# Second MLP product: running sums kept in PSUM banks instead of SBUF accumulators, and weight sums made by adding transfers

## The chip, the core and the metric

The kernel runs on one core of a Trainium2 chip. The metric is the device time of the kernel in microseconds (us); the kernel before was timed in three runs. A profile of one execution was taken beside these runs; its span goes from the first to the last instruction.

The engines are named as the profile names them: PE (TensorE) multiplies matrices into eight PSUM banks of 128 x 512 float32; DVE (VectorE) and ACT (ScalarE) read PSUM and SBUF; POOL (GpSimd) reads SBUF alone; SP issues transfers. Each engine works through its instructions in the order in which the program wrote them.

## The reference

One encoder layer over 1024 tokens of width 1024. What matters here is its last line, the squared-ReLU MLP with 4096 hidden channels:

```
u = RMSNorm(x)
...
x = x + m @ W_o
h = rms_norm(x, norm2_g) @ w_mlp_in            # 1024 x 4096
x = x + square(relu(h)) @ w_mlp_out            # back to 1024 x 1024
```

## The kernel before

All products run in float16 pieces: each operand is split into a high and a low part (ACT casts the high part, DVE computes the low part as the rest), and three passes (high x high, high x low, low x high) are summed in PSUM.

**The second MLP product.** The 4096 hidden channels are taken in four *chunks* s = 0 to 3. Each chunk is a product of 2 x 2 blocks by the Winograd form of Strassen's scheme: seven products o = 0 to 6 instead of eight. The running number is n = 7 s + o, 0 to 27. Each product has four *units* j = 0 to 3 of 128 tokens, and a unit is 12 matmuls of 512 columns into one PSUM bank (`unit`, line 210). The scheme's result blocks need sums of the products: with P0 to P6 the seven products in the order of the loop, X11 gets P0 + P2; X12 gets -(P0 + P1), P4 and P6; X22 gets -(P0 + P1 + P3) and P4; X21 gets P0 + P1 + P3 and P5.

**The operands (`prep2`).** For each product, operand set `ops` is prepared ahead in one of three buffers: ACT casts the activations `hf` (L1765, 128 x 2048), DVE makes their low part (L1767), ACT casts the weights (L1770, two of 128 x 1024), DVE makes their low parts (L1776, two of 128 x 1024). A `gate` holds the preparation of product n until the units of product n - 3 are in the program, so L1765 of product n waits until PE is done with product n - 3, and all of this preparation stands in DVE's order ahead of the reads of product n - 2. The preparation of product n also issues, on SP, the load of `hf` for product n + 3 (L1711). The weights of the seven products are w11, t2, w21, t3, t1, t4, w22: some are blocks of the weight matrix, some are sums of blocks, and the sums are made on POOL, as `tensor_tensor` additions: T2 = w12 + w22 + w11 (L1739, L1740), then in place w11 += w12 after product 0 is prepared (L1781), w12 += w22 after product 1 (L1785), T2 += w21 after product 3 (L1789).

**The results.** A unit's result is read out by its `post`, which the program writes after the matmuls of the *next* unit. The banks rotate: `anybank` hands out eight banks in turn, so seven other units stand between two that write the same bank. For o in 0, 1 and 3 the product goes to an accumulator in SBUF (`acc`, three of 128 x 4 x 512): in chunk 0 ACT copies it there (L1864), in chunks 1 to 3 DVE adds it there (L1866). For o in 2, 4, 5 and 6 DVE adds it straight into X1 (L1875), twice for o = 4. In chunk 3, `combine` adds the three accumulators to one another and into X1 on DVE and POOL (L1837 to L1846), and `SP.dma_start` writes the finished blocks out.

**What stands around the start of this stage.** The first MLP product (`quad` q = 0 to 15) ends just before. The last work on its hidden channels, `h_done` for q = 15, is Relu (L1623) and Square (L1625) on ACT, then on POOL the sums (L1345), and on DVE the maximum of a small row (L1640) and the steps of `pow2` (L108 to L113). The program writes L1640 before the first unit of product 0; the first three steps of `unit`'s loop then write L108, L110 and, between them, the two L1776 of product 2.

Of the kernel before, what the change touches and what calls it, by code (L numbers as in the profile page):

```python
# [10 lines left out]
F32 = mybir.dt.float32  # L11
# [3 lines left out]
AF = mybir.ActivationFunctionType  # L15
OP = mybir.AluOpType
# [36 lines left out]
def encoder_block(ctx: ExitStack, tc: tile.TileContext, x, weights, cols, gqk, rel, masks, out):  # L53
# [12 lines left out]
    def bank(tag):  # L66
        return psum.tile([128, 512], F32, name="ps_" + tag, tag=tag, bufs=banks[tag])
# [3 lines left out]

    rc = [0]

    def anybank():
        rc[0] += 1
        return bank("dsodsods"[rc[0] % 8])


    sc = base.tile([128, 512], F32, name="sc")
    sci = sc.bitcast(I32)  # L80
    area = {"keep": [0, 0, 144], "prep": [144, 144, 240], "tmp": [240, 240, 512]}

    def cols_of(kind, n):
        a = area[kind]
# [32 lines left out]
    fg, bg = [], []  # L117
# [9 lines left out]
    def step(n=1):  # L127
        for _ in range(n):
            for g in list(fg):
                if not advance(g):  # L130
                    fg.remove(g)
# [72 lines left out]
        V.tensor_scalar(sc[:, out], bk[:, 0:1], floor, None, op0=OP.max)  # L204
        yield

    def unit(mms, post=None, steps=0, ticks=0):

        for ps, l, r, a, b in mms:
            T.matmul(ps, l, r, start=a, stop=b)  # L210
        units[0] += 1
        work[0] += len(mms) * mms[0][0].shape[-1]
        settle()
        if post:
            late.append(post)
        for i in range(max(steps, ticks)):
            if i < steps:
                step()
            if i < ticks:
                tick()  # L220
# [228 lines left out]
    def group(ps, pairs):  # L449
        return [(ps, l, r, i == 0, i == len(pairs) - 1) for i, (l, r) in enumerate(pairs)]  # L450
# [318 lines left out]
    for n, (kind, b) in enumerate(todo):  # L769
# [6 lines left out]
        def post(ps=ps, kind=kind, n=n, ch=ch):  # L776
            fg.append(qk_vec(ps, ch.inv, kind, q16[n]))
# [840 lines left out]
    def h_done(q, c0=0, c1=512, wait1=0, wait2=0):  # L1618

        f = AS[q] if c1 < 512 else AS.pop(q)  # L1620
        v = f[:, :, c0:c1]
        yield from wait(wait1)
        A.activation(v[:, 0:4], v[:, 0:4], AF.Relu)  # L1623
        yield
        A.activation(v[:, 0:4], v[:, 0:4], AF.Square, scale=sc[:, c1w[q].inv],  # L1625
                     accum_out=sc[:, at(bsum[q // 4], 4 + q if c1 < 512 else q % 4)])
        yield
        yield from wait(wait2)
        if q > 1:
            yield from sums(v, G)  # L1630
        else:
            for _ in sums(v, V):
                pass
        if c1 < 512:
            return
        SP.dma_start(HS[q // 4][:, :, q % 4], f)
        live.remove(q)
        if q % 4 == 3:
            m = tmp()
            V.tensor_reduce(sc[:, m], sc[:, bsum[q // 4]], axis=AX, op=OP.max)  # L1640
            yield
            yield from pow2(m, 14, *R[q // 4])
            r_ready[q // 4] = True

    def quad(q, c0=0, c1=512):
# [69 lines left out]
    def prep2(s):  # L1715
# [19 lines left out]
            yield  # L1735
        sums = sum_of(sm)
        T2 = later["t2"]()
        for i in range(2):
            G.tensor_tensor(T2[:, i], w12[i], w22[i], op=OP.add)  # L1739
            G.tensor_tensor(T2[:, i], T2[:, i], w11[i], op=OP.add)  # L1740
        yield
        if s == 0:
            yield from gate(17)
# [3 lines left out]
        sw, inv = yield from scale_of(sums, 0)  # L1747
        fw = keep()
        mul(iR, sw, fw)
        c2[s].inv = inv  # L1750
        yield
        for o, (f, name) in enumerate(ORDER):
            n = 7 * s + o
            i = 16 + n
            yield from gate(i)
            pool, tag = TAGS[i % 3]
            if n > 1:
                OPS[i] = pool.tile([128, 2, 2, 2048], F16, name="ops", tag=tag)
            P = OPS[i]
            while ("h", n) not in later:  # L1760
                yield
            if 1 < n < 25:
                h_load(n + 3)
            hf = later.pop(("h", n)).rearrange("p k t -> p (k t)")
            A.activation(P[:, 1, 0], hf, AF.Copy, scale=sc[:, Rs])  # L1765
            yield
            V.scalar_tensor_tensor(P[:, 1, 1], hf, sc[:, Rs], P[:, 1, 0], op0=OP.mult, op1=OP.subtract)  # L1767
            w = {"w11": w11, "t1": w11, "t3": w12, "w21": w21, "w22": w22}.get(name) or [T2[:, i] for i in range(2)]
            for i2 in range(2):
                A.activation(P[:, 0, 0, 1024 * i2:1024 * i2 + 1024], w[i2], AF.Copy, scale=sc[:, fw])  # L1770
            yield
            while i == 17 and pe_done[0] < 16:
                yield
            for i2 in range(2):
                sl = slice(1024 * i2, 1024 * i2 + 1024)
                V.scalar_tensor_tensor(P[:, 0, 1, sl], w[i2], sc[:, fw], P[:, 0, 0, sl], op0=OP.mult, op1=OP.subtract)  # L1776
                yield
            ready.add(i)
            if name == "w11":
                for i2 in range(2):  # L1780
                    G.tensor_tensor(w11[i2], w11[i2], w12[i2], op=OP.add)  # L1781
                yield
            elif name == "t2":
                for i2 in range(2):
                    G.tensor_tensor(w12[i2], w12[i2], w22[i2], op=OP.add)  # L1785
                yield
            elif name == "t3":
                for i2 in range(2):
                    G.tensor_tensor(T2[:, i2], T2[:, i2], w21[i2], op=OP.add)  # L1789
                yield  # L1790
            elif name == "t1":
                done[0] += 4
                load_upto(done[0] + 5)
                if s < 3:
                    w2x_load(s + 1)
                    bg.append(prep2(s + 1))
            yield
# [22 lines left out]
    p4.close()  # L1820
    p5 = ExitStack()
    w5p = later["pool"] = p5.enter_context(tc.tile_pool(name="p5", bufs=1, reuse_waits="tile"))
    acc = {i: w5p.tile([128, 4, 512], F32, name=f"acc{i}") for i in (1, 6, 7)}
    t2 = w5p.tile([128, 2, 1024], F32, name="t2")
    later["t2"] = lambda: t2
    later["junk"] = w5p.tile([128, 2048], BF16, name="junk")

    combined = set()
    PLACE = {2: ((0, 0),), 4: ((4, 512), (0, 512)), 5: ((4, 0),), 6: ((0, 512),)}
    SUM = {0: 1, 1: 6, 3: 7}  # L1830

    def combine(j, o):

        x11, x12, x21, x22 = X1[:, j, :512], X1[:, j, 512:], X1[:, j + 4, :512], X1[:, j + 4, 512:]
        a1, a6, a7 = (acc[i][:, j] for i in (1, 6, 7))
        if o == 0:
            G.tensor_tensor(x11, x11, a1, op=OP.add)  # L1837
        elif o == 1:
            V.tensor_tensor(a6, a6, a1, op=OP.add)
            yield  # L1840
            G.tensor_tensor(x12, x12, a6, op=OP.subtract)
        else:
            V.tensor_tensor(a7, a7, a6, op=OP.add)
            yield
            G.tensor_tensor(x22, x22, a7, op=OP.subtract)
            V.tensor_tensor(x21, x21, a7, op=OP.add)  # L1846
        combined.add((j, o))
        yield

    for n in range(28):  # L1850
        s, o = n // 7, n % 7
        need(16 + n)
        P = OPS.pop(16 + n)
        inv = c2[s].inv
        for j in range(4):
            bk = anybank()
            for c, m in ((0, 256), (256, 256)) if n == 27 and j == 3 else ((0, 512),):
                ps = bk[:, c:c + m]

                def post(ps=ps, j=j, o=o, s=s, c=c, m=m, inv=inv):  # L1860
                    if o in SUM:
                        t = acc[SUM[o]][:, j]
                        if s == 0:
                            A.activation(t, ps, AF.Copy, scale=sc[:, inv])  # L1864
                        else:
                            V.scalar_tensor_tensor(t, ps, sc[:, inv], t, op0=OP.mult, op1=OP.add)  # L1866
                        if s == 3:
                            fg.append(combine(j, o))
                        return
                    before = {2: 0, 4: 3, 5: 3, 6: 1}[o]  # L1870
                    while s == 3 and (j, before) not in combined:
                        step()
                    for b, d in PLACE[o]:
                        t = X1[:, b + j, d + c:d + c + m]
                        V.scalar_tensor_tensor(t, ps, sc[:, inv], t, op0=OP.mult, op1=OP.add)  # L1875
                    if s == 3:
                        b, d = PLACE[o][0]
                        r = (b + j) * 128
                        SP.dma_start(out[r:r + 128, d + c:d + c + m], X1[:, b + j, d + c:d + c + m])

                unit(group(ps, [(P[:, 1, sa, 512 * k + 128 * j:512 * k + 128 * j + 128],
                                 P[:, 0, sw, 512 * k + c:512 * k + c + m]) for k in range(4) for sa, sw in PASSES]),
                     post, 2, 4)
        pe_done[0] = 17 + n
    settle()
    p5.close()
# [57 lines left out]
```

## Time and profile before

| | |
|---|---|
| device time, median of 3 runs (lowest, highest) | 1208.2 us (1207.58, 1208.48) |
| the profiled execution: span | 1205.3 us |
| what lies between its span and the median of the runs | 2.9 us |
| first matmul of the second MLP product | 911.12 us |
| last unit of it (24 matmuls of 256 columns) | starts at 1198.69 us |
| busy in the span | PE 1188.0, DVE 938.7, ACT 759.8, POOL 433.1 us |

The page lists no device time of the profiled execution apart from its span; sums are made against the span, and the 2.9 us are carried along to speak of the median.

In a row of the timeline stand: start and length in us, engine, line, operation, output and inputs with their shapes, the number of merged instructions, and in brackets how long the engine sat idle before and what released it. In a row of the table by windows stand: the window, its length, then for PE, PEld, DVE, ACT and POOL the busy us and the number of instructions, then the granted clock of PE, the share of the DMA engines and GB/s.

### The profile page before, as it was taken

Reading aid. Unit: us, or ns where it says so; the run is one execution under the profiler, and the core shown is the slowest. Engines: PE = TensorE matmul, PEld = TensorE weight load, DVE = VectorE, ACT = ScalarE, POOL = GpSimd, SP = SyncE. Lnnn points to the kernel's source line nnn. Section 1 sums busy time; section 2 is a strip of 40 time slices with the busy share of each in tenths; the row PEclk is TensorE's granted clock in tenths of the full one; section 3 lists DMA queues with packets and bytes.
Section 4 is the critical chain, followed back from the end, with each engine's and each line's share of the span. In section 5 each row is a group of like instructions: output and inputs, shape, how many; then the busy total and the mean of one; then the engine's idle time right before and its main releaser. Section 6 shows DMA issues by size and latency. Waiting matters only on the chain.

```text
span 1205.3 us, 17076 instructions
## 1 busy us (share of the span) xinstructions
PE 1188.0 (99%) x6294; PEld 573.8 (48%) x6294; DVE 938.7 (78%) x1759; ACT 759.8 (63%) x1183; POOL 433.1 (36%) x280
## 2 busy tenths in 40 slices
PE   6999999999999999999999999999999999999998
PEld 4444445555444444444467444444444444444444
DVE  7777988988368787877878655545548999999997
ACT  7766679867554545337779778678676744746440
POOL 1640011222311112001004465565567471553662
PEclk9999999999999999999999999999999999999999
DMA  7766657676542211224386545445465925334202
GB/s 264 151 213 141 140 119 130 133 146 123 103 123 65 67 56 53 70 93 187 57 155 183 182 159 192 149 139 193 145 247 201 352 97 217 129 138 194 105 35 105
DMA packets 171012, 173.36 MB, mean 144 GB/s; under 512 B 131504, under 2 KB 132016, under 8 KB 166832
## 3 DMA queue, kind: packets, MB, share of 16 engines
q1 hardware_dynamic: 170352, 168.07, 47.9%
q10 hardware_dynamic: 576, 4.19, 0.8%
q8 instruction: 49, 0.80, 0.3%
q14 instruction: 35, 0.29, 0.1%
HBM read 102.51 MB, written 37.75 MB: 116 GB/s over the span
## 4 chain that ended last, share of the span: by engine, by line
PE 73%; DVE 9%; ACT 1%; issue 1%; DMA 1%; DVEq 0%; ACTq 0%
PE ps_d L210 26%; PE ps_s L210 23%; PE ps_o L210 16%; PE ps_d L1039 6%; DVE w_s L1163 2%; PE ps_o L1016 1%; PE ps_s L959 1%; DVE sg L1279 1%; DVE P L999 1%; DMA u2T<-v 1%; DVE sz L973 1%; ACT w_s L1167 0%; DVE sc L317 0%; DVE m L1281 0%; ACT sg L1245 0%
## 5 line engine op out<-in xcount | busy, mean ns | idle before, releaser
L210 PEld LDWEIGHTS <-ops 128*128 128x128 f16 x1356 | 132.4, 98 | 157.3
L210 PEld LDWEIGHTS <-w 128*128 128x128 f16 x1368 | 132.8, 98 | 140.0 <-DMA u2T<-v 0.6
L1039 PE MATMUL ps_d<-uT,w_ws 128*128 128x512 f16 x528 | 123.7, 379 | 0.1
L210 PE MATMUL ps_d<-ops 128*128 128x512 f16 (+1 forms) x528 | 118.3, 374 | 0.0
L1765 ACT ACTIVATE ops<-hf,sc 128x2048 f16<-128x2048 f32 x26 | 52.0, 2000 | 97.9 <-PE ps_o L210 35.2
L210 PE MATMUL ps_s<-ops 128*128 128x512 f16 x492 | 112.9, 379 | 0.0
L1152 POOL TENSOR_TENSOR tsum<-raw 128x512 f32<-128x512 f32 x28 | 46.0, 1658 | 149.6 <-ACT raw L1138 141.6
L1345 POOL TENSOR_TENSOR as<-as 128x512 f32<-128x512 f32 x56 | 77.5, 1384 | 39.3 <-ACT as L1625 36.0
L210 PEld LDWEIGHTS <-w_s 128*128 128x128 f16 x588 | 56.8, 98 | 69.4 <-DVE w_s L1163 1.9
L210 PE MATMUL ps_d<-u2x,w 128*128 128x512 f16 (+1 forms) x360 | 80.0, 372 | 0.0
L210 PEld LDWEIGHTS <-uT 128*128 128x128 f16 x504 | 49.0, 98 | 59.6 <-DMA uT<-u 0.8
L1039 PEld LDWEIGHTS <-w_ws 128*128 128x128 f16 x528 | 51.2, 98 | 54.5 <-DVE cv L861 0.4
L210 PE MATMUL ps_o<-ops 128*128 128x512 f16 x336 | 77.1, 379 | 0.0
L1767 DVE SCALAR_TENSOR_TENSOR ops<-hf,sc,ops 128x2048 f16<-128x2048 f32 x26 | 74.0, 2846 | 3.7 <-ACT ops L1765 3.7
L210 PE MATMUL ps_o<-u2T,w 128*128 128x512 f16 (+1 forms) x324 | 71.7, 371 | 0.0
L1138 ACT ACTIVATE raw<-raw,sc 128x256 f32<-128x256 f32 x172 | 71.0, 493 | 0.8 <-DMA raw<-in_weights 0.7
L1152 POOL TENSOR_TENSOR gsum<-raw 128x512 f32<-128x512 f32 x14 | 19.0, 1376 | 133.0 <-issue 72.8
L1167 ACT ACTIVATE w<-raw,sc 128x512 f16<-128x512 f32 (+1 forms) x28 | 24.6, 927 | 54.1 <-DVE sc L426 54.1
L297 DVE SCALAR_TENSOR_TENSOR w_ws<-raw,sc,w_ws 128x512 f16<-128x512 f32 (+2 forms) x72 | 51.2, 763 | 4.7 <-ACT w_ws L306 4.7
L1658 DVE TENSOR_TENSOR as<-ps_d,as 128x512 f32<-128x512 f32 (+1 forms) x14 | 9.4, 672 | 55.8 <-ACT as L1677 53.4
L210 PE MATMUL ps_s<-u2T,w 128*128 128x512 f16 (+1 forms) x252 | 52.7, 359 | 0.0
L982 ACT ACTIVATE sz<-sz,sc 128x384 f32<-128x384 f32 (+1 forms) x64 | 37.2, 582 | 22.5 <-DVE sc L973 15.0
(357 smaller groups left out, 2629.5 us busy)
## 6 DMA issues: line engine op xcount, KB each, us to landing
raw<-in_weights SPq DMA_DIRECT2D x88, 512.0 KB, 5.4
hs<-as SPq DMA_DIRECT2D x16, 1792.0 KB, 8.7
hf<-hs SPq DMA_DIRECT2D x26, 1024.0 KB, 6.3
w2x<-in_weights SPq DMA_DIRECT2D x16, 512.0 KB, 8.1
raw<-in_weights SPq DMA_DIRECT2D x16, 384.0 KB, 3.5
xt<-in_x SPq DMA_DIRECT2D x8, 512.0 KB, 10.0
gs<-s ACTq DMA_DIRECT2D x4, 1024.0 KB, 4.0
x<-in_x SPq DMA_DIRECT2D x8, 512.0 KB, 9.8
```

What stands on the lines that cost most here:

```text
L210: T.matmul(ps, l, r, start=a, stop=b)
L297: V.scalar_tensor_tensor(lo, self.raw[p][:, o:o + m], sc[:, c:c + 1], hi, op0=OP.mult, op1=OP.subtract)
L959: T.matmul(ps[:, :nb * 128], QD[:, p, e, w, i * 128:(i + 1) * 128], KD[:, 2 * p + e, lo * 128:(lo + nb) * 128], start=w == 0, stop=w == 1)
L982: A.activation(z, z, AF.Exp, scale=-1.0, bias=sc[:, d["mx"]], accum_out=sc[:, d["sm"]])
L1039: T.matmul(ps, l, r, start=a, stop=b)
L1138: A.activation(v, v, AF.Copy, scale=sc[:, at(g, 4 * i + k)])
L1152: G.tensor_tensor(t[:, o], a, b, op=OP.add)
L1163: V.scalar_tensor_tensor(o(1), w, sc[:, s], o(0), op0=OP.mult, op1=OP.subtract)
L1167: A.activation(o(0), w, AF.Copy, scale=sc[:, s])
L1345: sub.tensor_tensor(z[o], z[a], z[b], op=op)
L1765: A.activation(P[:, 1, 0], hf, AF.Copy, scale=sc[:, Rs])
L1767: V.scalar_tensor_tensor(P[:, 1, 1], hf, sc[:, Rs], P[:, 1, 0], op0=OP.mult, op1=OP.subtract)
```

## The change

- `eight` takes all eight banks once. Four of them, `chain[0]` to `chain[3]`, are kept for the running sum of unit j: products o = 0, 1, 3 and 5 of a chunk are all summed there (only o = 0 starts the bank anew), and each partial sum is read in between: P0 into X11, P0 + P1 into X12, P0 + P1 + P3 into X22 (both with the negated scale), all four into X21. The other four banks rotate among products 2, 4 and 6, and the small sum of `scale_of`.
- The accumulators, `combine` and the copies of chunk 0 on ACT go. All reads are L1875's operation on DVE, in all four chunks: 4 for each product, 8 for o = 4.
- In chunks 1 to 3 the weight sums are made by transfers that add to their destination, issued on POOL's queue: T2 begins as a load of w12 (SP), to which w22 and then w11 are added; the other sums are one adding transfer for each half. Chunk 0 keeps POOL's additions.
- One scale is smaller by a factor of 2 (`pow2(m, 13, ...)`), and a column with the negated scale is computed for each chunk.

```diff
+    fixed = []
+
     def anybank():
         rc[0] += 1
-        return bank("dsodsods"[rc[0] % 8])
+        return fixed[rc[0] % len(fixed)] if fixed else bank("dsodsods"[rc[0] % 8])
...
-    def unit(mms, post=None, steps=0, ticks=0):
+    def unit(mms, post=None, steps=0, ticks=0, free=False):
 
         for ps, l, r, a, b in mms:
-            T.matmul(ps, l, r, start=a, stop=b)
+            T.matmul(ps, l, r, start=a, stop=b, skip_group_check=free)
...
-            yield from pow2(m, 14, *R[q // 4])
+            yield from pow2(m, 13, *R[q // 4])
...
         T2 = later["t2"]()
-        for i in range(2):
-            G.tensor_tensor(T2[:, i], w12[i], w22[i], op=OP.add)
-            G.tensor_tensor(T2[:, i], T2[:, i], w11[i], op=OP.add)
+
+        def add(o, w):
+            for i in range(2):
+                if s == 0:
+                    G.tensor_tensor(o[i], o[i], w[i], op=OP.add)
+                else:
+                    G.dma_start(o[i], w[i], accum_op=OP.add)
+
+        t2 = [T2[:, i] for i in range(2)]
+        if s == 0:
+            for i in range(2):
+                G.tensor_tensor(t2[i], w12[i], w22[i], op=OP.add)
+                G.tensor_tensor(t2[i], t2[i], w11[i], op=OP.add)
+        else:
+            for i in range(2):
+                load_into(t2[i], c2[s], 2 + i)
+            yield
+            add(t2, w22)
+            add(t2, w11)
         yield
...
-        c2[s].inv = inv
+        c2[s].inv, c2[s].neg = inv, cols_of("neg", 1)
+        V.tensor_scalar(sc[:, c2[s].neg], sc[:, inv], -1.0, None, op0=OP.mult)
...
             if name == "w11":
-                for i2 in range(2):
-                    G.tensor_tensor(w11[i2], w11[i2], w12[i2], op=OP.add)
+                add(w11, w12)
                 yield
             elif name == "t2":
-                for i2 in range(2):
-                    G.tensor_tensor(w12[i2], w12[i2], w22[i2], op=OP.add)
+                add(w12, w22)
                 yield
             elif name == "t3":
-                for i2 in range(2):
-                    G.tensor_tensor(T2[:, i2], T2[:, i2], w21[i2], op=OP.add)
+                add(t2, w21)
                 yield
...
-    acc = {i: w5p.tile([128, 4, 512], F32, name=f"acc{i}") for i in (1, 6, 7)}
...
+    PLACE = {0: ((0, 0, 1),), 1: ((0, 512, 0),), 2: ((0, 0, 1),), 3: ((4, 512, 0),), 4: ((4, 512, 1), (0, 512, 1)),
+             5: ((4, 0, 1),), 6: ((0, 512, 1),)}
+    LAST = {2: (0, 0), 4: (4, 512), 5: (4, 0), 6: (0, 512)}
+    eight = [anybank() for _ in range(8)]
+    chain = eight[:4]
+    fixed[:] = eight[4:]
+
+    def step2(n, j):
+        s, o = n // 7, n % 7
+        P, c = OPS[16 + n], c2[s]
+        bk = chain[j] if o in (0, 1, 3, 5) else anybank()
+        for c0, m in ((0, 256), (256, 256)) if n == 27 and j == 3 else ((0, 512),):
+            ps = bk[:, c0:c0 + m]
+
+            def post(ps=ps, c0=c0, m=m):
+                for b, d, plus in PLACE[o]:
+                    t = X1[:, b + j, d + c0:d + c0 + m]
+                    V.scalar_tensor_tensor(t, ps, sc[:, c.inv if plus else c.neg], t, op0=OP.mult, op1=OP.add)
+                if s == 3 and o in LAST:
+                    b, d = LAST[o]
+                    r = (b + j) * 128
+                    SP.dma_start(out[r:r + 128, d + c0:d + c0 + m], X1[:, b + j, d + c0:d + c0 + m])
+
+            mms = group(ps, [(P[:, 1, sa, 512 * k + 128 * j:512 * k + 128 * j + 128],
+                              P[:, 0, sw, 512 * k + c0:512 * k + c0 + m]) for k in range(4) for sa, sw in PASSES])
+            if o in (0, 1, 3, 5):
+                mms = [(p, l, r, a and o == 0, b) for p, l, r, a, b in mms]
+            unit(mms, post, 2, 4, o in (0, 1, 3, 5))
...
         for j in range(4):
...
+            step2(n, j)
```

More of the change, by code (lines that the diff above doesn't have):

```diff
@@ L72, in encoder_block @@
     rc = [0]
+    fixed = []
     def anybank():
         rc[0] += 1
-        return bank("dsodsods"[rc[0] % 8])
-    sc = base.tile([128, 512], F32, name="sc")
+        return fixed[rc[0] % len(fixed)] if fixed else bank("dsodsods"[rc[0] % 8])
+    sc = base.tile([128, 520], F32, name="sc")
     sci = sc.bitcast(I32)
-    area = {"keep": [0, 0, 144], "prep": [144, 144, 240], "tmp": [240, 240, 512]}
+    area = {"keep": [0, 0, 144], "prep": [144, 144, 240], "tmp": [240, 240, 512], "neg": [512, 512, 520]}
     def cols_of(kind, n):
@@ L1826, in encoder_block @@
     later["junk"] = w5p.tile([128, 2048], BF16, name="junk")
[L1828 to L1848, printed above, removed]
+    PLACE = {0: ((0, 0, 1),), 1: ((0, 512, 0),), 2: ((0, 0, 1),), 3: ((4, 512, 0),), 4: ((4, 512, 1), (0, 512, 1)),
[23 more added lines that the diff above has]
+            unit(mms, post, 2, 4, o in (0, 1, 3, 5))
     for n in range(28):
@@ L1852, in encoder_block @@
         need(16 + n)
-        P = OPS.pop(16 + n)
-        inv = c2[s].inv
         for j in range(4):
[L1856 to L1883, printed above, removed]
+            step2(n, j)
+        OPS.pop(16 + n)
         pe_done[0] = 17 + n
```

## The prediction

> **What bounds the kernel now.** I read the page's first part, then the table by windows over the second MLP product, then the timeline of each engine there.
>
> ```profile
> span 1205.3 us, 17076 instructions
> PE 1188.0 (99%) x6294; PEld 573.8 (48%) x6294; DVE 938.7 (78%) x1759; ACT 759.8 (63%) x1183; POOL 433.1 (36%) x280
> ```
> ```profile
> 911.12:921.48 10.36, 10.36 (x49) 4.67 (x48) 10.33 (x9) 4.89 (x4) 9.00 (x3) 1.00 1.02 348
> 921.48:931.84 10.36, 10.36 (x49) 4.70 (x48) 6.94 (x9) 10.33 (x11) 4.82 (x3) 1.00 0.29 122
> 1050.00:1100.00 50.00, 50.00 (x233) 22.65 (x232) 47.81 (x37) 20.53 (x16) 27.73 (x9) 1.00 0.51 195
> ```
>
> In each window PE is busy for the whole length at a granted clock of 1.00: 50 us hold 233 matmuls, 0.2146 us each, and a product of 48 takes 10.36 us. The stage has no idle PE to win back. DVE is almost as full (47.81 of 50), so what DVE does late can only cost.
>
> The tail gives nothing either:
>
> ```profile
> 1201.51 0.88 DVE L1875 SCALAR_TENSOR_TENSOR x<-ps_d,sc,x 128x256 f32<-128x256 f32 x2 [1.87 <-PE ps_d L210]
> ```
>
> DVE waited for PE (1.87 us) before the last two reads, and the changed kernel ends in the same way: product 6 of chunk 3, two half reads, two stores. So the change is worth what it adds in PE waits.
>
> **Part 1: the kept bank at the start.** Before, a bank came back after seven other units. Now unit j of product 1 adds into the bank of unit j of product 0, three units later, and its first matmul must wait until DVE has read that bank. The work around this place:
>
> ```profile
> 911.12 2.75 PE L210 MATMUL ps_s<-ops 128*128 128x512 f16 x12
> 918.78 2.00 ACT L1765 ACTIVATE ops<-hf,sc 128x2048 f16<-128x2048 f32 x1 [4.21 <-DMA hf<-hs]
> 920.68 2.17 ACT L1770 ACTIVATE ops<-w2x,sc 128x1024 f16<-128x1024 f32 x2
> 921.48 2.75 PE L210 MATMUL ps_d<-ops 128*128 128x512 f16 x12
> 922.76 1.90 ACT L1623 ACTIVATE as<-as 128x2048 f32<-128x2048 f32 x1
> 924.69 2.00 ACT L1625 ACTIVATE as<-as,sc 128x2048 f32<-128x2048 f32 x1
> 926.69 0.67 ACT L1864 ACTIVATE acc<-ps_s,sc 128x512 f32<-128x512 f32 x1
> 926.82 0.16 DVE L1640 TENSOR_REDUCE sc<-sc 128x1 f32<-128x4 f32 x1 [3.35 <-ACT as L1625]
> 926.86 8.97 POOL L1345 TENSOR_TENSOR as<-as 128x512 f32<-128x512 f32 x4 [6.74 <-ACT as L1625]
> 927.08 2.13 DVE L1776 SCALAR_TENSOR_TENSOR ops<-w2x,sc,ops 128x1024 f16<-128x1024 f32 x1
> 929.20 2.23 DVE L1776 SCALAR_TENSOR_TENSOR ops<-w2x,sc,ops 128x1024 f16<-128x1024 f32 x1
> 931.35 0.14 DVE L112 TENSOR_SCALAR sc<-sc 128x1 int32<-128x1 int32 x1
> ```
> ```profile
> L1875 DVE SCALAR_TENSOR_TENSOR x<-ps_s,sc,x 128x512 f32<-128x512 f32 x31 | 22.3, 739 | 0.0
> ```
>
> Product 0 starts at 911.12 and product 1 at 921.48. The read of unit 0 was a copy on ACT (L1864, 926.69), already 5 us behind, and the rotation hid it. Now it is on DVE, and its place in DVE's order follows from the program: L1640 is written before the first unit, the loop behind that unit writes L108, L1776, L110, L1776, the second unit writes the read and then L112. The trace shows L1640, L1776, L1776, L112 in this order. L1640 cannot start before 926.82: it waits for L1625, which stands behind L1623, L1770 and L1765 on ACT, and that one waited 4.21 us for the load of `hf`. The change touches none of these. The two L1776 end at 929.20 + 2.23 = 931.43 (slowed by POOL's L1345, which stays), the read takes 0.74: 932.2. PE stands from 921.48 to 932.2: **10.7 us**. The other reads follow at once (the units are long done), so there is one wait, not four.
>
> Does anything give it back? No: the stage behind it runs at PE's pace. It does cover one term: chunk 0's twelve copies leave ACT and come to DVE as 12 x 0.739 = 8.9 us. DVE had 10.36 - 6.94 = 3.4 us free in the window of product 1, and PE's wait gives it 10.7 more; so 0, and up to 8.9 - 3.4 = 5.5 if that cover were gone.
>
> **Part 2: the clock after the wait.**
>
> ```profile
> 12.86 1.03 PE L525 MATMUL ps_o<-ident,u 128*128 128x128 f16 x8
> 15.15 1.03 PE L525 MATMUL ps_o<-ident,u 128*128 128x128 f16 x8
> 18.64 0.61 PE L525 MATMUL ps_o<-ident,u 128*128 128x128 f16 x8
> 1203.00:1205.30 2.30, 0.00 (x0) 0.00 (x0) 0.00 (x0) 0.00 (x0) 0.00 (x0) 0.84 0.28 95
> ```
>
> At the start of the kernel eight equal matmuls take 1.03 us, at 18.64 they take 0.61: PE starts slow. The last row shows a mean clock of 0.84 over the final 2.3 us: if it fell to half, it did so 0.74 us before the end, about 3 us after the last matmul. A wait of 10.7 us is longer. By these rows the slow time lasts at least from 12.86 to 16.2 (3.3 us) and at most to 18.64 (5.8 us); at half speed half of it is lost, 1.7 to 2.9. I take **2.3 us**, the middle, with 0 as the lower bound (no drop). The Trainium skill's "TensorE: Matmul & The Clock Gate" (Part 1: The HAM clock gate) says that about 3.4 us without work halve the clock and about 3.4 us of work restore it; that would cost 1.7 us and make the sum 12.4 instead of 13.0.
>
> **Part 3: the kept banks in chunks 1 to 3.** The same three-unit distance returns at products 8, 15 and 22.
>
> ```profile
> 976.70 7.69 POOL L1781 TENSOR_TENSOR raw<-raw 128x1024 f32<-128x1024 f32 x2 [7.16 <-DVE ops L1776]
> 982.11 6.66 DVE L1776 SCALAR_TENSOR_TENSOR ops<-t,sc,ops 128x1024 f16<-128x1024 f32 x2
> 990.95 7.69 POOL L1789 TENSOR_TENSOR t<-t,w2x 128x1024 f32<-128x1024 f32 x2
> 993.06 6.67 DVE L1776 SCALAR_TENSOR_TENSOR ops<-w2x,sc,ops 128x1024 f16<-128x1024 f32 x2
> 994.03 2.32 PE L210 MATMUL ps_o<-ops 128*128 128x512 f16 x10
> 994.23 2.00 ACT L1765 ACTIVATE ops<-hf,sc 128x2048 f16<-128x2048 f32 x1 [6.28 <-PE ps_s L210]
> ```
>
> (That last row is the pattern of every product: ACT starts 0.2 us after PE frees the buffer.)
>
> ```profile
> 999.65 0.74 DVE L1866 SCALAR_TENSOR_TENSOR acc<-ps_s,sc,acc 128x512 f32<-128x512 f32 x1
> 1002.28 2.34 DVE L1767 SCALAR_TENSOR_TENSOR ops<-hf,sc,ops 128x2048 f16<-128x2048 f32 x1
> 1004.54 2.47 DVE L1776 SCALAR_TENSOR_TENSOR ops<-raw,sc,ops 128x1024 f16<-128x1024 f32 x2
> 1066.57 1.67 PE L210 MATMUL ps_o<-ops 128*128 128x512 f16 x7
> 1073.03 0.74 DVE L1866 SCALAR_TENSOR_TENSOR acc<-ps_d,sc,acc 128x512 f32<-128x512 f32 x1
> ```
>
> At before's pace the change would pay here too: product 8 starts at 994.03 and the read of product 7's first unit ends at 1000.4, 6.4 us late; product 15 starts at 1066.57, the read ends at 1073.8, 7.2 late. But the lateness comes from POOL: beside its additions two L1776 take 6.66, alone 2.47. In chunks 1 to 3 POOL adds nothing any more. Then DVE needs, from the start of a product, 0.2 + 2.0 (ACT) + 2.34 + 2.47 + 0.74 = 7.75 us to the read, under 10.36. So **0**, with 2.6 us to spare; if DVE is not relieved, 6.4 + 7.2 (product 22 not counted). DVE's count in these chunks hardly moves: the twelve L1866 of a chunk become twelve reads of the same size, and `combine` goes. The other distances stay at seven units. The column with the negated scale is one more short DVE step like L112 (0.14) per chunk.
>
> **Part 4: the adding transfers.** No row shows one.
>
> ```profile
> hf<-hs SPq DMA_DIRECT2D x26, 1024.0 KB, 6.3
> DMA to landing us min/median/max: 4.6/6.3/15.6
> 1019.25 2.47 DVE L1776 SCALAR_TENSOR_TENSOR ops<-t,sc,ops 128x1024 f16<-128x1024 f32 x2
> 1023.94 2.35 POOL L1739 TENSOR_TENSOR t<-raw,w2x 128x1024 f32<-128x1024 f32 x1 [25.30 <-DMA w2x<-in_weights]
> ```
>
> The tightest is T2 of chunk 2. SP must wait for the last reader of the old T2 (1019.25 + 2.47 = 1021.7) and then loads 1 MB, about 6.3 us: 1028. Behind that waiting load on SP stand only loads of `hf` for products three ahead. Two adding steps of 1 MB follow; call one A. They wait in POOL's queue, where only further sums are queued. T2 is due when it starts to hold up the first read of product 14: from 1066.57 count back that read and the three reads before it (4 x 0.74), the preparation between (2.34 + 2.47) and T2's own two low parts with ACT's casts (2.47 and about 1): 1055.3. So 2 A may be 27 us, A 13.6. A plain MB takes 4.6 to 15.6 here. I take A = 10, above the plain median because the destination is read as well: **0**. At A = 15.6 chunks 2 and 3 pay 4 us each, 8 in all; at A = 20, 13 each. Chunk 1 has its own fresh tile and starts earlier. The skill's "Collectives: The Full Stack" (The bandwidth ceiling) says that an adding transfer has two reads for one write and runs at half a copy's rate; twice the plain median is an estimated 12.6, still no wait, and no run here shows it yet.
>
> **Sum.** 10.7 + 2.3 + 0 + 0 = 13.0 us on a span of 1205.3: 1218.3. The median of the runs before, 1208.2, lies 2.9 above the span; with that, **1221.2 us**. About 0.2% (2.4 us) is what a measurement of this kernel can tell from no change.
>
> **Rivals.**
> *Slow adding transfers.* For: nothing in the trace prices them, and they share the engines with loads that already took up to 15.6 us. Against: slack of two products. With A of 16 to 20 the sum is 1221.2 + 8 to 26, and at the ends where ACT waits too, more: some 1229 to 1250. It decides from A = 13.6.
> *DVE is not relieved*: POOL's issuing of transfers slows DVE as its additions did. For: the same two engines slow each other in the rows above. Against: the slow rows stand beside additions on POOL, and the adds themselves leave it. Then the waits of part 3 come, 13.6 us, each with a slow clock behind it (2 x 2.3): 1239.
> *Not slower: the wait does not come.* If the read of product 0's first unit went ahead of L1640 in DVE's order, it could run at 914 plus the queue in front of it, before 921.48, and PE would never stand: 1208.2, and faster only if some PE idle were removed, of which the stage has none. It decides on whether the read ends before 921.48. Against: the program's order and the four DVE rows above.
>
> **How the numbers follow.** Main case 0.65: its own range is 1218.9 (no clock drop) to 1224. Slow transfers 0.18, DVE not relieved 0.09, no wait 0.08. The range 1217 to 1240 leaves out the last and the far end of the slow transfers. Slower 0.92, same 0.05, faster 0.03.
>
> **What would show it.** A PE gap of about 10.7 us in front of product 1's first matmul, released by DVE's read of the first kept bank, and near 932 a window with a granted clock under 1.00. In chunks 1 to 3: no PE gap, two L1776 at 2.5 us, almost no POOL time, and DVE with idle time. Wrong would be: no gap at product 1 (part 1 falls); gaps before products 8, 15, 22 released by DVE (part 3), or by ACT or DVE waiting for an adding transfer (part 4).

## The result

| | median | lowest to highest |
|---|---|---|
| before | 1207.89 us | 1207.02 to 1208.48 (4 runs) |
| changed | 1220.16 us | 1219.25 to 1222.38 (4 runs) |

The changed kernel is slower by a ratio of 1.0107 (95% interval 1.0093 to 1.0121), 12.3 us. The forecast was 1221.2 us. The profiled execution of it has a span of 1218.4 us. In its code lines have moved: `unit` is L212, the preparation of operands L1784 to L1795, the read of a bank L1860, the maximum L1642, Square of `h_done` L1627, the adding transfers L1746.

The first part of its page, to be read against the same two lines of before:

```profile
span 1218.4 us, 17128 instructions
PE 1190.5 (98%) x6294; PEld 574.5 (47%) x6294; DVE 893.6 (73%) x1763; ACT 752.7 (62%) x1171; POOL 335.1 (28%) x268
```

DVE lost 45 us of work and POOL 98, and the span still grew by 13.1. PE's busy time grew by only 2.5 with the same number of matmuls: so PE mostly *stood*. Where, the timeline of the changed kernel at the start of the stage shows (here and below, rows between those shown are left out):

```profile
911.38 2.75 PE L212 MATMUL ps_s<-ops 128*128 128x512 f16 x12
918.59 2.00 ACT L1784 ACTIVATE ops<-hf,sc 128x2048 f16<-128x2048 f32 x1 [3.76 <-DMA hf<-hs]
919.15 2.75 PE L212 MATMUL ps_s<-ops 128*128 128x512 f16 x12
924.50 2.00 ACT L1627 ACTIVATE as<-as,sc 128x2048 f32<-128x2048 f32 x1
926.63 0.16 DVE L1642 TENSOR_REDUCE sc<-sc 128x1 f32<-128x4 f32 x1 [2.89 <-ACT as L1627]
926.89 2.13 DVE L1795 SCALAR_TENSOR_TENSOR ops<-w2x,sc,ops 128x1024 f16<-128x1024 f32 x1
929.01 2.22 DVE L1795 SCALAR_TENSOR_TENSOR ops<-w2x,sc,ops 128x1024 f16<-128x1024 f32 x1
931.15 0.74 DVE L1860 SCALAR_TENSOR_TENSOR x<-ps_s,sc,x 128x512 f32<-128x512 f32 x1
931.99 4.69 PE L212 MATMUL ps_s<-ops 128*128 128x512 f16 x12 [10.09 <-issue]
936.52 2.75 PE L212 MATMUL ps_o<-ops 128*128 128x512 f16 x12
```

Product 0 starts at 911.38, so product 1 would start 10.36 later, at 921.74; it starts at 931.99, 0.1 us after the read of the first kept bank ended. That is a wait of 10.25 us. (Waits are counted here from the moment at which PE would have started its next unit, 2.59 us after the last one began; the number in a row's bracket is 0.16 shorter, as the profile lets a unit end 2.75 after its start. The profile could not name the releaser and writes "issue"; the row above it, and the experiments, name it.) The unit behind the wait takes 4.53 us to the start of the next, 1.94 more than the usual 2.59. The table by windows of the changed kernel says why, in the column of the granted clock:

```profile
921.90:923.00 1.10, 0.00 (x0) 0.00 (x0) 1.10 (x1) 1.10 (x2) 0.00 (x0) 1.00 1.05 439
925.00:926.00 1.00, 0.00 (x0) 0.00 (x0) 0.00 (x0) 1.00 (x1) 0.00 (x0) 0.85 0.02 8
928.00:932.00 4.00, 0.01 (x1) 0.04 (x2) 3.96 (x6) 2.57 (x3) 3.90 (x2) 0.50 0.00 0
932.00:934.00 2.00, 2.00 (x5) 0.69 (x6) 2.00 (x4) 0.00 (x0) 1.92 (x3) 0.50 0.01 4
934.00:936.00 2.00, 2.00 (x6) 0.73 (x5) 2.00 (x2) 0.00 (x0) 2.00 (x2) 0.51 0.55 206
936.00:938.00 2.00, 2.00 (x10) 0.88 (x9) 2.00 (x1) 0.00 (x0) 2.00 (x2) 1.00 1.04 389
950.00:1200.00 250.00, 250.00 (x1163) 113.34 (x1161) 189.99 (x215) 120.68 (x105) 26.29 (x30) 1.00 0.74 214
```

While PE stands the clock falls to 0.50, and it stays there for the first 4 us of work. From 950 to 1200 PE is busy without a gap at 1.00, as it was before. 10.25 + 1.94 = 12.2 us, the difference of the medians. The two profiled spans differ by 13.1: in the changed kernel's, the stage started 0.26 later, and 0.66 more lies behind the start of the last unit, a part whose cause was not looked for.

### The profile page after: what moved, and what is told of

Same layout as the page of the kernel before. It is cut to its first block, busy times and chain, and to the rows that moved or that the text cites. A ratio compares the mean times of both kernels' runs of the same rounds, so it can differ in the third digit from the quotient of the medians.

```text
span 1218.4 us, 17128 instructions
## 1 busy us (share of the span) xinstructions
PE 1190.5 (98%) x6294; PEld 574.5 (47%) x6294; DVE 893.6 (73%) x1763; ACT 752.7 (62%) x1171; POOL 335.1 (28%) x268
## 4 chain that ended last, share of the span: by engine, by line
PE 69%; DVE 8%; issue 3%; ACT 2%; POOL 2%; DMA 2%; SPq 0%; DVEq 0%; POOLq 0%; ACTq 0%
PE ps_d L212 23%; PE ps_s L212 21%; PE ps_o L212 15%; PE ps_d L1041 7%; DVE w_s L1165 2%; PE ps_o L1018 1%; PE ps_s L961 1%; POOL as L1347 1%; DMA hf<-hs 1%; DVE sg L1281 1%; DMA u2T<-v 1%; DVE P L1001 1%; ACT w_s L1169 0%; DVE sz L975 0%; POOL h L1752 0%
## 5 line engine op out<-in xcount | busy, mean ns | idle before, releaser
L212 PEld LDWEIGHTS <-ops 128*128 128x128 f16 x1356 | 132.8, 98 | 169.1 <-issue 13.2
L212 PEld LDWEIGHTS <-w 128*128 128x128 f16 x1368 | 132.8, 98 | 140.4 <-DMA u2T<-v 0.9
L212 PE MATMUL ps_s<-ops 128*128 128x512 f16 x528 | 121.6, 383 | 10.1 <-issue 10.1
L1784 ACT ACTIVATE ops<-hf,sc 128x2048 f16<-128x2048 f32 x26 | 51.9, 1998 | 122.8 <-PE ps_s L212 88.7
L212 PE MATMUL ps_d<-ops 128*128 128x512 f16 x480 | 108.5, 379 | 0.0
L212 PEld LDWEIGHTS <-w_s 128*128 128x128 f16 x588 | 56.8, 98 | 69.4 <-DVE w_s L1165 1.9
L212 PE MATMUL ps_d<-u2x,w 128*128 128x512 f16 (+1 forms) x360 | 80.0, 372 | 0.0
L1786 DVE SCALAR_TENSOR_TENSOR ops<-hf,sc,ops 128x2048 f16<-128x2048 f32 x26 | 62.9, 2418 | 23.1 <-ACT ops L1784 21.8
L212 PE MATMUL ps_o<-ops 128*128 128x512 f16 (+1 forms) x348 | 77.1, 372 | 0.0
L212 PEld LDWEIGHTS <-uT 128*128 128x128 f16 x504 | 49.0, 98 | 59.5 <-DMA uT<-u 0.7
L212 PE MATMUL ps_o<-u2T,w 128*128 128x512 f16 (+1 forms) x324 | 71.7, 371 | 0.0
L212 PE MATMUL ps_s<-u2T,w 128*128 128x512 f16 (+1 forms) x252 | 52.7, 359 | 0.0
L1860 DVE SCALAR_TENSOR_TENSOR x<-ps_s,sc,x 128x512 f32<-128x512 f32 x48 | 35.3, 745 | 22.2 <-PE ps_s L212 22.2
```

Of the source, the lines that this page charges most:

```text
L212: T.matmul(ps, l, r, start=a, stop=b, skip_group_check=free)
L1860: V.scalar_tensor_tensor(t, ps, sc[:, c.inv if plus else c.neg], t, op0=OP.mult, op1=OP.add)
```

## The experiments

Three theories stood. A: the loss is PE's wait for one read, set by the place of that read in DVE's order, and the slow clock behind it. B: it lies in the adding transfers and their load on the DMA engines. C: DVE carries too much in chunk 0 since ACT's twelve copies moved to it. The first four runs shared one set of runs of the kernel before (1207.34 us), the last four another (1207.50).

**Moving the read forward: three runs.** The first writes the maximum and the steps behind it later:

```diff
         if q % 4 == 3:
+            if q == 15:
+                yield from wait(9)
             m = tmp()
```

> The changed kernel with one step moved: the maximum of the last row of the first MLP product (and the steps behind it) is written on DVE nine steps later, behind the reads of product 0. Theory A (the loss is PE's wait for the read of product 0's first unit, set by the read's place in DVE's order, and the slow clock behind it): ahead of the read now stand the low parts of product 2 alone, so it ends about 926.9 instead of 931.9; PE waits 5.2 us instead of 10.25, long enough for the clock to fall (1 to 1.9 us): 1214 to 1215. Theory B (the loss lies in the adding transfers and their load on the DMA engines): nothing moves, 1220. Theory C (DVE carries too much in chunk 0 since the twelve copies moved to it): nothing moves, 1220.

Measured: 1214.83 us, ratio 1.0060 (1.0047 to 1.0072). The second keeps this and also takes the preparation of product 2's weights out of the way:

```diff
-            unit(mms, post, 2, 4, o in (0, 1, 3, 5))
+            unit(mms, post, 2, 0 if (n, j) == (0, 0) else 4, o in (0, 1, 3, 5))
```

> As the run before, and the low parts of product 2's weights are written on DVE behind the first read too. Theory A: ahead of the read stands only the low part of product 2's activations, it ends about 924.5; PE waits 2.8 to 4 us, about the time after which the clock falls: 1210.7 to 1213. Theories B and C: 1220.

Measured: 1211.95 us, ratio 1.0035 (1.0022 to 1.0047). The third, with the late maximum too, writes product 0's units first (in `step2` of this version the last two numbers say how many steps of preparation follow a unit; here none do):

```diff
     settle()
-    tick(6)
...
+    need(16)
+    step2(0, 0, 0, 0)
+    step2(0, 1, 0, 0)
+    tick(3)
+    need(17)
+    step2(0, 2, 0, 0)
+    step2(0, 3, 0, 0)
     while live:
         step()
...
-        for j in range(4):
+        for j in range(4 if n else 0):
             step2(n, j)
```

> The units of product 0 are written before the preparation of product 1 is finished, so the first read stands right behind the last reads of the first MLP product, and the other reads of product 0 before the preparation of product 2; the maximum stays late. All arithmetic is as in the changed kernel. Theory A: the first read ends about 917, PE waits for product 1's weights at most 0.7 us, no slow clock: 1208.0 to 1208.8, the time of the kernel before. Theories B and C: 1220.

Measured: 1207.86 us, ratio 1.0003 (0.9995 to 1.0012): no difference from before is left. The timelines of the first and the second of the three, at the first read and the wait:

```profile
925.40 0.74 DVE L1862 SCALAR_TENSOR_TENSOR x<-ps_s,sc,x 128x512 f32<-128x512 f32 x1
926.24 5.28 PE L212 MATMUL ps_s<-ops 128*128 128x512 f16 x12 [4.97 <-ACT as L1627]
931.31 2.99 PE L212 MATMUL ps_o<-ops 128*128 128x512 f16 x12
```
```profile
923.25 0.74 DVE L1862 SCALAR_TENSOR_TENSOR x<-ps_s,sc,x 128x512 f32<-128x512 f32 x1
924.09 4.39 PE L212 MATMUL ps_s<-ops 128*128 128x512 f16 x12 [2.57 <-issue]
928.32 2.75 PE L212 MATMUL ps_o<-ops 128*128 128x512 f16 x12
```

Each time PE starts 0.1 us after the read ends. (In the first the profile names L1627 as releaser: that had ended earlier, and it is the read that came last.) Counted as above, the waits are 5.1 and 2.7. In the first, the two slow units cost 2.5 and 0.2 more than 2.59 each; in the second, the slow unit costs 1.6. That makes 7.9 and 4.4 us, against 7.5 and 4.6 in the medians. The third's timeline has no wait at all:

```profile
916.77 0.74 DVE L1852 SCALAR_TENSOR_TENSOR x<-ps_s,sc,x 128x512 f32<-128x512 f32 x1
917.43 5.25 DVE L1797 SCALAR_TENSOR_TENSOR ops<-h,sc,ops 128x1024 f16<-128x1024 f32 x2
920.34 5.34 PE L212 MATMUL ps_s<-ops 128*128 128x512 f16 x24
922.60 0.74 DVE L1852 SCALAR_TENSOR_TENSOR x<-ps_o,sc,x 128x512 f32<-128x512 f32 x1
925.52 2.75 PE L212 MATMUL ps_o<-ops 128*128 128x512 f16 x12
```

The first read ends at 917.5, ahead of the low parts of product 1's weights (L1797), and two units (x24) run through the border between the products, at 922.9. B and C fall: the transfers and the twelve reads on DVE are all still there.

**The clock alone.** 44 more matmuls into a free bank, whose result nobody reads, fill most of the wait.

```diff
+        if n == 0:
+            need(17)
+            for i in range(44):
+                T.matmul(fixed[0], OPS[17][:, 1, 0, 0:128], OPS[17][:, 0, 0, 0:512], start=True, stop=True)
         OPS.pop(16 + n)
```

> The changed kernel with 44 more matmuls of 512 columns between product 0 and product 1, into a bank that is free (9.5 us of PE work in the wait of 10.25). Theory A: the wait stays but PE is idle under 1 us, the clock stays at 1.00, and only the 1.9 us of slow matmuls go: 1218.2. Rival: the 1.9 us behind the wait are not the clock's (they belong to the waiting itself, or to loads of weights): 1220.2.

Measured: 1218.41 us, ratio 1.0089 (1.0075 to 1.0102), with this in its timeline and its table by windows:

```profile
921.95 9.66 PE L1880 MATMUL ps_d<-ops 128*128 128x512 f16 x44
931.84 0.74 DVE L1860 SCALAR_TENSOR_TENSOR x<-ps_s,sc,x 128x512 f32<-128x512 f32 x1
932.63 2.75 PE L212 MATMUL ps_s<-ops 128*128 128x512 f16 x12 [1.03 <-DVE sc L114]
```
```profile
932.00:934.00 2.00, 1.37 (x7) 0.65 (x7) 1.97 (x5) 0.00 (x0) 1.92 (x2) 1.00 0.02 4
```

The wait is where it was, behind the same read, the clock stays at 1.00, and the unit behind the wait has its usual length of 2.75. Against before 1.2 us less are lost than in the changed kernel (11.1 instead of 12.3); the two intervals overlap, so the times alone do not prove it. The traces say why it is less than 1.9: the 1.94 of slow clock are gone, but product 1, due at 921.95, starts at 932.63, a wait of 10.7 instead of 10.25, as the read came later. The row of the clock is what settles it.

**The weight sums back on POOL.** `add` and the first sum of T2 use `tensor_tensor` in all chunks (`if s >= 0:` for both `if s == 0:`).

> The changed kernel with the weight sums of chunks 1 to 3 back on POOL as additions, no adding transfers. Theory A: DVE is slow beside POOL's additions as before, so the first reads of products 7, 14 and 21 come late again: by the trace of before 6.4, 7.2 and 1.6 us after product 8, 15 and 22 want their bank, 15 us on top of 1220.2, and up to 2 us of slow clock behind each of the two long waits: 1235 to 1239. Rival (the three-unit distance costs only in chunk 0, since PE's wait there lets DVE catch up): 1220.

Measured: 1244.08 us, ratio 1.0302 (1.0288 to 1.0317). The PE waits in chunks 1 to 3, and one of the DVE rows ahead of the first, in its timeline:

```profile
1011.30 5.16 PE L212 MATMUL ps_s<-ops 128*128 128x512 f16 x12 [5.82 <-DVE x L1860]
1092.24 5.28 PE L212 MATMUL ps_s<-ops 128*128 128x512 f16 x12 [5.82 <-DVE x L1860]
1173.66 4.21 PE L212 MATMUL ps_s<-ops 128*128 128x512 f16 x12 [5.82 <-DVE x L1860]
```
```profile
1001.74 7.68 POOL L1744 TENSOR_TENSOR t<-t,w2x 128x1024 f32<-128x1024 f32 x2
1003.85 6.65 DVE L1795 SCALAR_TENSOR_TENSOR ops<-w2x,sc,ops 128x1024 f16<-128x1024 f32 x2
```

The mechanism of theory A is there, but not its size, and the time lies above the expected 1235 to 1239: three equal waits of 5.82 (6.0 counted as above) instead of 6.4, 7.2 and 1.6, and slow units (4.2 to 5.3 instead of 2.75) behind each of them. The waits are 17.9 and the slow clock behind them 6.8, together 24.7 us. The span grew by 22.9 over that of the changed kernel, because 1.8 came off elsewhere: the stage started 0.7 earlier, product 1's wait and slow clock were 0.5 shorter, and 0.7 less lies at the end. Why the waits are equal was not tested: probably each lets DVE catch up, so that each chunk starts alike, where before its lateness was carried on. So with DVE's work in this order the kept banks need POOL's additions out of the way, as the adding transfers put them.

**The transfers alone.** In the kernel before, only the sums of chunks 1 to 3 become adding transfers (the diff's lines around `add` and no others).

> The kernel before with only the weight sums of chunks 1 to 3 by adding transfers; accumulators and rotating banks as before. Theory A: PE was never waiting, so nothing to win and nothing lost: 1207 to 1208.5, with DVE's busy time in the stage lower by some 40 us. Rival (the transfers themselves cost, by the load on the DMA engines or at the end of the kernel, where the changed kernel's profile has 0.7 us more behind the last read): 1209 to 1212.

Measured: 1208.05 us, ratio 1.0003 (0.9994 to 1.0012). Its window from 950 to 1200, and below it the same window of before:

```profile
950.00:1200.00 250.00, 250.00 (x1169) 113.86 (x1167) 198.28 (x219) 118.11 (x104) 45.46 (x42) 1.00 0.76 220
```
```profile
950.00:1200.00 250.00, 250.00 (x1169) 113.93 (x1168) 236.82 (x219) 117.88 (x104) 122.44 (x42) 1.00 0.39 145
```

DVE falls from 236.82 to 198.28 us with the same 219 instructions, the DMA share nearly doubles, and the time does not move: PE was full before and is full now.

**How far the transfers may be late.** T2 gets one more adding step (`add(t2, w22)` once more), then two more (`add(t2, w11)` as well). T2 is then another sum than the scheme needs, so these two versions no longer compute the layer; they only show what a longer row of transfers does to the time.

> The changed kernel with one more adding step of 1 MB in T2's row of transfers in chunks 1 to 3 (three steps instead of two, so T2 is another sum). A step takes about 8.2 us here; T2 of chunk 2 is complete near 1057.6 and by the prediction's count back due near 1067.8. Theory A (slack of about 10 us): 8.2 us later, still no wait: 1220 to 1221. Rival (T2 is already just in time, as the slack was counted back from single rows): some 8 us in each chunk, 1240 and more.

> As the run before with two more adding steps (four instead of two). Theory A: 16.4 us later against a slack of 10 in chunks 1 and 2 and 12.7 in chunk 3: waits of about 6, 6 and 4 us before products 8, 15 and 22, with a slow clock behind each: 1236 to 1242. Rival (the slack is larger, because DVE, relieved, has more idle time than the count back gave it): 1220.

Measured: 1220.12 us, ratio 1.0104 (1.0091 to 1.0118) with one, and 1239.78 us, ratio 1.0280 (1.0251 to 1.0308) with two. With one, PE has no wait in chunks 1 to 3, though in chunk 2 ACT waits for the second half of T2:

```profile
1067.63 1.15 ACT L1790 ACTIVATE ops<-t,sc 128x1024 f16<-128x1024 f32 x1 [5.70 <-DMA t<-w2x]
```

The timeline of the second, with the waits of PE and what was late in chunk 2:

```profile
1013.49 4.74 PE L212 MATMUL ps_s<-ops 128*128 128x512 f16 x12 [6.80 <-DVE x L1862]
1094.39 5.25 PE L212 MATMUL ps_s<-ops 128*128 128x512 f16 x12 [6.20 <-DVE x L1862]
```
```profile
1084.48 1.15 ACT L1791 ACTIVATE ops<-t,sc 128x1024 f16<-128x1024 f32 x1 [2.86 <-DMA t<-raw]
1085.67 1.28 DVE L1797 SCALAR_TENSOR_TENSOR ops<-t,sc,ops 128x1024 f16<-128x1024 f32 x1 [2.73 <-ACT ops L1791]
1093.50 0.74 DVE L1862 SCALAR_TENSOR_TENSOR x<-ps_s,sc,x 128x512 f32<-128x512 f32 x1
```

One more step is free, two are not. In chunk 2, from the start of the first adding step to ACT's cast of the second half of T2, it takes 26.6 us with three steps (1041.07 to 1067.63) and 34.7 with four (1049.82 to 1084.48). The waits are 6.8 and 6.2 where 6 and 6 were expected. Chunk 3 was expected to wait 4 us and lost 0.3; there the four steps took 30.6 us (1129.16 to 1159.77). Waits and slow clock of chunks 1 and 2 together are 17.8 us, and the spans differ by 17.6 (1236.0 against 1218.4). The medians differ by 19.6: the profiled run was the fastest of four that scatter from 1237.8 to 1248.0, and this scatter is not explained.

## Why the prediction was right

*Part 1, the wait at product 1:* forecast 10.7, measured 10.25. The order L1642, L1795, L1795, read stands in the trace as it was worked out, and the three moved versions follow it in order: 10.25, 5.1, 2.7 and no wait for reads that end at 931.9, 926.1, 924.0 and in time. The 0.45 are a stage that started 0.26 later and a read that ended 0.3 earlier, with 0.1 between its end and PE's start. The cover of the twelve copies turned out not to be needed: without any wait (the third version) they still cost nothing, where the prediction had allowed up to 5.5.

*Part 2, the clock:* 2.3 forecast, 1.94 measured. The slow time, taken as 3.3 to 5.8 us, was 4.0 (931.99 to about 935.96, by the 0.51 of the window from 934), and half of it is lost. Over the runs with one wait the loss is 1.6 to 2.7. "TensorE: Matmul & The Clock Gate" of the Trainium skill (Part 1: The HAM clock gate) gave 1.7 by its 3.4 us of work; both values lie inside. Its 3.4 us without work is not what every trace here shows: the clock fell about 3.8 us after the last matmul in the changed kernel, but 2.5 after it in the second moved version.

*Part 3, the kept banks in chunks 1 to 3:* no wait, with 2.6 us to spare by the sum of single rows. In the changed kernel's timeline the first read of product 14 ends at 1076.3, and product 15 starts with the second half of the x24 below, 2.59 after its first, at 1079.0: 2.7 to spare. The second row shows DVE relieved as assumed.

```profile
1075.55 0.75 DVE L1860 SCALAR_TENSOR_TENSOR x<-ps_s,sc,x 128x512 f32<-128x512 f32 x1
1073.16 2.48 DVE L1795 SCALAR_TENSOR_TENSOR ops<-w2x,sc,ops 128x1024 f16<-128x1024 f32 x2
1076.43 5.34 PE L212 MATMUL ps_s<-ops 128*128 128x512 f16 x24
```

The rival "DVE is not relieved" falls with it, though its place was right: the POOL version shows such a DVE at work, 24.7 us instead of the forecast 18.2 (13.6 of waits and 4.6 of clock). Products 8 and 15 cost 17.3 of them; product 22, left out of that sum, costs 7.4.

*Part 4, the adding transfers:* A was taken as 10 between 4.6 and 15.6. In the changed kernel's timeline the second step of T2 in chunk 2 begins 8.2 us after the first for one half of T2, 9.5 for the other:

```profile
1041.50 0.86 POOL L1746 DMA_DIRECT2D t<-w2x  x1 [37.35 <-DMA t<-in_weights]
1042.99 0.88 POOL L1746 DMA_DIRECT2D t<-w2x  x1 [0.63 <-DMA t<-in_weights]
1049.70 0.87 POOL L1746 DMA_DIRECT2D t<-raw  x1 [5.84 <-DMA t<-w2x]
1052.47 0.86 POOL L1746 DMA_DIRECT2D t<-raw  x1 [1.90 <-DMA t<-w2x]
```

The twice-a-copy of the Trainium skill's "Collectives: The Full Stack" (The bandwidth ceiling), 12.6 by the estimate, was too slow for this case: a step took 8.2 to 9.5 us, where a plain load of 1 MB (`hf`) had a median of 8.1 in the same execution. The page states its rule for the adding step of a ReduceScatter, whose ring uses two DMA engines. The bound of 13.6 for each of two steps, 27 us in all, held too: rows that took 26.6 and 34.7 us bracket it.

*The rival "no wait"* needed the read ahead of L1640. It is what the third moved version makes, and it gave the time forecast for it, that of before.

*Luck, and the term that was off.* The sum for the span was 1218.3 and the span is 1218.4, but not for the reasons in the sum: PE's wait and the clock made 12.2 instead of 13.0, and 0.9 that the sum did not have made up for it (0.26 ahead of the stage, 0.66 at the end). The miss of 1.0 in the median is all in the 2.9 us carried from span to median: in the changed kernel's profiled run the two lie 1.7 apart (1218.4 and 1220.14).

No version came out faster than the kernel before, and the profiles say why none of these could: its PE has no idle time in this stage.

## What to carry to other kernels

A bank that is kept for a running sum comes back sooner than one in rotation; find the shortest distance, and read from the trace where the read of that bank stands in its engine's order, not how long it takes. A foreign step that waits ahead of such a read is paid for by PE (here a maximum over four columns, waiting for ACT, made 5.1 of the 10.25 us; the work on operands ahead of the read made the rest), and engines that have idle time on the average do not help. Where PE is full, work taken off DVE and POOL buys slack and no time; spend it on something, or leave it.

## What the runs showed of the hardware

A short wait already halves the clock. In the second moved version PE stood for only 2.7 us, and its table by windows reads:

```profile
923.50:924.09 0.59, 0.00 (x0) 0.03 (x1) 0.59 (x2) 0.59 (x1) 0.00 (x0) 0.95 0.79 333
924.09:925.00 0.91, 0.91 (x3) 0.36 (x4) 0.91 (x1) 0.88 (x2) 0.00 (x0) 0.50 0.14 54
927.00:928.00 1.00, 1.00 (x5) 0.44 (x4) 1.00 (x3) 1.00 (x1) 0.92 (x2) 0.78 0.00 0
```

The clock fell just before PE came back, some 2.5 us after the last matmul, and returned in the window from 927 on: 1.6 us lost on a wait of 2.7. The moment is not fixed: in the changed kernel the 0.85 in the window from 925 puts it at about 925.7, 3.8 us after the last matmul. The prediction had read "about 3 us" from the end of the kernel. A wait of 1.03 us, in the run with the added matmuls, left the clock alone.

Issuing transfers from POOL did not slow DVE, where additions on POOL did: two L1795 took 2.47 us beside the issues at 1041.50 and 1042.99 (part 4 above), and 6.65 beside the additions of the POOL version.

```profile
1042.06 2.47 DVE L1795 SCALAR_TENSOR_TENSOR ops<-w2x,sc,ops 128x1024 f16<-128x1024 f32 x2
```
